# The delta-rule inverse recorded in closed stretches on VectorE, with later filler instructions tied behind its end

## The chip, the core and the metric

One core of one Trainium2 chip runs the whole program. The metric is the device time of one execution in microseconds (us); the time of the kernel before is the median of three runs. Five engines work side by side, each through a queue of its own and in the order in which the program puts them there: PE (TensorE, matrix products), DVE (VectorE), ACT (ScalarE), POOL (GpSimd) and SP (which issues DMAs). An engine goes on to its next instruction only when the semaphores that this instruction waits for have arrived, so an instruction that waits also holds up everything behind it in its queue.

## What is computed

Two transformer blocks on 256 tokens of width 1024. The second block has a gated delta rule with four heads of 128, beside a pooling branch, and after it a layer that picks 16 of 16384 experts for each head (the top-k). What the change touches is the delta rule. For each chunk and head the reference inverts a unit lower triangular matrix made from keys, decays and gates, and uses the inverse in everything that follows:

```python
q = _l2norm(qkv[..., :DN_WIDTH].reshape(b, s, DN_HEADS, DN_HEAD_DIM))
k = _l2norm(qkv[..., DN_WIDTH:2 * DN_WIDTH].reshape(b, s, DN_HEADS, DN_HEAD_DIM))
...
a_mat = jnp.where(strict, jnp.einsum("bhnid,bhnjd->bhnij", k_beta, k) * decay, 0.0)
t_mat = lax.linalg.triangular_solve(eye + a_mat, jnp.broadcast_to(eye, a_mat.shape),
                                    left_side=True, lower=True)
w_vals = jnp.einsum("bhnij,bhnjd->bhnid", t_mat, v_beta)
...
v_new = wv - jnp.einsum("bhcd,bhde->bhce", kcd, state)
o = jnp.einsum("bhcd,bhde->bhce", qd, state) + jnp.einsum("bhij,bhje->bhie", attn_c, v_new)
```

The kernel works with two chunks of 128 tokens (`tb` 0 and 1) and four heads, so eight 128x128 matrices `N`.

## The kernel before

Weights come from HBM in tiles of 128x1024 fp32 (512 KB). `Stream` turns each into two tiles: `whi` (an ACT copy, L218) and `wlo` (raw minus `whi`, on DVE, L231). A projection then is 24 matmuls (8 slices, three products each, L374 to L376) with 256 columns. There are five tile pairs in this stage and four raw tiles; a raw tile is loaded again only when its `wlo` has been written.

The delta stage, from about 430 to 550 us, weaves two strands together. The **main strand** (`main`, L1502) is the delta rule itself. The **filler** (`filler`, L1445) is the work beside it: sixteen projections, in the order q, v, p (pooling) and z with four heads each, every one followed on DVE by an evacuation from PSUM (`ct`, L1302, `pp`, L1434, `zt`, L1415), three convolution taps (L1306) for q and v, and a last product (L1295). The projections' outputs go through three PSUM buffers, `pb`; the main strand's go through four, `pa`. `weave` (L272) runs a piece of `main` up to its next `yield`, takes from the yielded number how much filler is due, and runs that much of `filler`. This decides the order in which instructions are recorded and their priority; a list scheduler that knows dependences and priorities then puts each engine's queue in order, so an instruction recorded later can still stand earlier.

The main strand in its own order, with the lines that the prediction speaks of:

1. the decays `dec` (L1512 on PE, L1517 and L1518 on ACT), masked on POOL (L1519, L1545);
2. the sums of squares of the keys (squares L525 on ACT, L1377 on PE) and their inverse root `yk` (`rsqrt_steps`, L408: three DVE steps, then three Newton rounds, with `eng=G` on POOL, L442 to L445, four instructions each);
3. `byk` (L1530), its spread over partitions by PE (L463), the products k by k (L1535), the matrix `N` (L1541, L1544) on DVE;
4. `inverse16` (L606): the diagonal 16x16 blocks `dg` (L619 to L623 on DVE), their rows copied to all partitions by PE and ACT (`rep`, L630 and L632), fifteen forward substitution steps on DVE ("the solve", L637 and L640), and the block diagonal `Z` (L644 on ACT, L646 on DVE);
5. three rounds that double the inverted blocks (L1563, L1574 on PE, L1579 and L1584 on DVE), the products with q (L1593), the transposes of v and k (L1615, L1619), and the state and outputs (L1476, L1627, L1631, L1637, L1498, L1645, L1646);
6. the output projection of the pooling branch, which is filler too, from the first matmul of `yah` on; then the tail of the stage.

## Time and profile before

| | us |
|---|---|
| median of three runs (1387.05 to 1393.6) | 1387.48 |
| the profiled execution | 1386.37 |
| its span in the trace | 1384.3 |
| PE busy | 1337.0 |
| DVE busy | 993.3 |
| ACT busy | 678.5 |

The span is what the trace covers; the execution's own time is 2.07 us longer. A PE that is shown busy may still be at half its clock, so the granted clock (1.00 is 2.4 GHz, 0.50 is 1.2 GHz) is read beside it. The trace shows the end of a matmul only as a model of the pipeline; the distance from one start to the next is what a matmul costs in a row of them.

### The profile page before, as it was taken

What the parts mean: (1) busy time and instruction counts of PE and PEld (TensorE: products, weight loads), DVE (VectorE), ACT (ScalarE), POOL (GpSimd) and SP (SyncE); (2) the same over time, 40 slices, a digit from 0 to 9 for tenths busy, and PEclk for the clock granted to TensorE, in tenths of its full rate; (3) what the DMA queues carried; (4) which work ended last, traced back from release to release, by engine and by line L of the source; (5) the groups of instructions that cost most, each with busy time, mean ns of one, the idle gap of its engine ahead of it and who ended that gap; (6) DMA issues with size and microseconds to landing.
All of it is one profiled execution on the core that took longest, in us unless ns stands there. A gap on an engine that the chain in (4) does not pass through costs nothing.

```text
span 1384.3 us, 26929 instructions
## 1 busy us (share of the span) xinstructions
PE 1337.0 (97%) x10570; PEld 1252.3 (90%) x10570; DVE 993.3 (72%) x2088; ACT 678.5 (49%) x1248; POOL 238.1 (17%) x230
## 2 busy tenths in 40 slices
PE   7989999999999968999999999999999999999998
PEld 6888988999989968999999999999998888888886
DVE  7865777898878975699995777888865555545554
ACT  3522455565565531465554554444444554554454
POOL 4611242100014610200000000000012222222221
PEclk9899999999999989999999999999999999999999
DMA  6241443565543311445555454545456555555553
GB/s 227 55 112 48 130 145 122 190 228 183 184 152 112 130 64 33 138 151 178 180 182 175 158 164 158 167 157 165 164 187 198 191 190 197 196 189 194 197 193 111
DMA packets 64335, 217.89 MB, mean 157 GB/s; under 512 B 10273, under 2 KB 11249, under 8 KB 64081
## 3 DMA queue, kind: packets, MB, share of 16 engines
q1 hardware_dynamic: 59376, 212.76, 46.1%
q0 software_dynamic: 992, 2.72, 0.7%
q8 instruction: 83, 1.36, 0.4%
q10 hardware_dynamic: 3840, 0.70, 0.4%
q14 instruction: 44, 0.35, 0.1%
HBM read 214.70 MB, written 1.44 MB: 156 GB/s over the span
## 4 chain that ended last, share of the span: by engine, by line
PE 86%; DVE 7%; ACT 3%; POOL 2%; issue 1%; DMA 1%; ACTq 0%; DVEq 0%; POOLq 0%
PE pa L1943 25%; PE pb L374 14%; PE pb L375 14%; PE pb L376 14%; PE pa L375 3%; PE pa L374 3%; PE pa L376 3%; PE pc L1897 1%; PE pb L1897 1%; PE pa L1574 1%; ACT whi L218 1%; DVE wlo L231 1%; PE pa L1064 1%; PE pb L1831 0%; PE pc L471 0%
## 5 line engine op out<-in xcount | busy, mean ns | idle before, releaser
L218 ACT ACTIVATE whi<-raw 128x1024 fp32r<-128x1024 f32 x396 | 418.3, 1058 | 509.4 <-PE pb L375 248.0
L231 DVE TENSOR_TENSOR wlo<-raw,whi 128x1024 fp32r<-128x1024 f32 x382 | 472.2, 1237 | 247.4 <-ACT whi L218 246.1
L374 PE MATMUL pb<-xnh,whi 128*128 128x256 f32 x1024 | 294.8, 288 | 0.0
L375 PE MATMUL pb<-xnl,whi 128*128 128x256 f32 x1024 | 290.1, 283 | 0.0
L376 PE MATMUL pb<-xnh,wlo 128*128 128x256 f32 x1024 | 289.5, 283 | 0.0
L1943 PE MATMUL pa<-whi,up 128*128 128x512 f32 x1024 | 274.7, 390 | 0.0
L1943 PEld LDWEIGHTS pa<-whi,up 128*128 128x128 f32 x1024 | 192.2, 188 | 39.8
L375 PEld LDWEIGHTS pb<-xnl,whi 128*128 128x128 f32 x1024 | 196.3, 192 | 0.0
L374 PEld LDWEIGHTS pb<-xnh,whi 128*128 128x128 f32 x1024 | 196.1, 192 | 0.0
L376 PEld LDWEIGHTS pb<-xnh,wlo 128*128 128x128 f32 x1024 | 196.0, 192 | 0.0
L374 PE MATMUL pb<-xh,whi 128*128 128x256 f32 x648 | 187.4, 289 | 0.0
L375 PE MATMUL pb<-xl,whi 128*128 128x256 f32 x648 | 184.8, 285 | 0.1
L376 PE MATMUL pb<-xh,wlo 128*128 128x256 f32 x648 | 184.9, 285 | 0.0
L1943 PE MATMUL pa<-wlo,up 128*128 128x512 f32 x512 | 158.4, 389 | 0.0
L511 POOL TENSOR_TENSOR up<-hb,up 128x256 fp32r<-128x256 f32 x32 | 45.9, 1435 | 553.8 <-ACT up L510 553.8
L374 PEld LDWEIGHTS pb<-xh,whi 128*128 128x128 f32 x648 | 124.1, 191 | 0.9 <-ACT xh L576 0.2
L375 PEld LDWEIGHTS pb<-xl,whi 128*128 128x128 f32 x648 | 123.9, 191 | 0.8 <-DVE xl L577 0.3
L376 PEld LDWEIGHTS pb<-xh,wlo 128*128 128x128 f32 x648 | 123.6, 191 | 0.5 <-DVE wlo L231 0.2
L1943 PEld LDWEIGHTS pa<-wlo,up 128*128 128x128 f32 x512 | 96.2, 188 | 19.9
L511 POOL TENSOR_TENSOR up<-scr,up 128x256 fp32r<-128x256 f32 x32 | 47.1, 1472 | 127.0 <-ACT up L510 127.0
L231 POOL TENSOR_TENSOR wlo<-raw,whi 128x1024 fp32r<-128x1024 f32 x19 | 46.4, 2448 | 45.1 <-ACT whi L218 35.2
L375 PE MATMUL pa<-al,whi 128*128 128x256 f32 x176 | 49.1, 281 | 0.0
(541 smaller groups left out, 2207.1 us busy)
## 6 DMA issues: line engine op xcount, KB each, us to landing
raw<-down SPq DMA_DIRECT2D x128, 512.0 KB, 3.3
raw<-up SPq DMA_DIRECT2D x128, 512.0 KB, 3.3
raw<-w_in SPq DMA_DIRECT2D x46, 512.0 KB, 3.4
raw<-w_up SPq DMA_DIRECT2D x44, 512.0 KB, 3.4
raw<-w_down SPq DMA_DIRECT2D x22, 512.0 KB, 3.4
raw<-w_out SPq DMA_DIRECT2D x16, 512.0 KB, 3.3
raw<-w_query SPq DMA_DIRECT2D x16, 512.0 KB, 3.4
x<-xT SPq DMA_DIRECT2D x4, 256.0 KB, 5.5
```

The costliest lines, as they stand in the source:

```text
L218: nc.scalar.activation(hi, self.raw[self.nh], AF.Copy)
L231: e.tensor_tensor(lo[:, a:z], raw[:, a:z], hi[:, a:z], ALU.subtract)
L374: mm(ps, w[0], x[0], start=start, stop=False, **k)
L375: mm(ps, w[0], x[1], start=False, stop=False, **k)
L376: mm(ps, w[1], x[0], start=False, stop=stop, **k)
L511: (eng or self.nc.vector).tensor_tensor(lo, src, hi.bitcast(F32), ALU.subtract)
L1064: mm(out[h, q], lh[h, 8 * hf + q, 0:64], self.halves(rh[h, 8 * hf + q, :], l, odd), start=True, stop=True)
L1574: mm(out[:, h], lh[:, tb * 4 + h, :], self.halves(rh[:, tb * 4 + h, :], l, odd), start=True, stop=True)
L1897: mm(ps[:, n, :], e1[:, q, :, r], eg[m][:, q, :, r], start=(m == 0), stop=(m == 1))
L1943: mm(acc[tb * 2 + hf], a[:, ts], b[:, hf * 512:hf * 512 + 512], start=False, stop=(e == 127 and lo == 1), skip_group_check=True)
```

## The change

`rsqrt_steps` loses its POOL variant, and `main` calls the DVE variant without yielding, as one piece; one `yield` after the k by k products goes too. The fifteen solve steps are one piece, with a single `yield` behind them where there were fifteen. `inverse16` keeps the last DVE instruction of two stretches (`self.blocks`: the sum that ends `dg`, then the last reduction of the solve), and `weave` records each piece of filler that follows inside `tc.issue_after` of that instruction: every DVE instruction of such a piece gets an order behind it. Other engines' instructions get none. The first entry of `YL`, the filler due after each piece of `head`, goes from 0.2 to 0.45. No arithmetic changes but the form of the Newton rounds.

```diff
-YL = [0.2, 0.64, 1.60, 3.20, 0.64, 0.72, 0.48, 0.80, 0.40, 1.92, 1.20, 0.16]
+YL = [0.45, 0.64, 1.60, 3.20, 0.64, 0.72, 0.48, 0.80, 0.40, 1.92, 1.20, 0.16]
...
-def weave(tc, main, fill, engines="", lead=None, leads=None):
+def weave(tc, main, fill, engines="", lead=None, leads=None, behind=None):
...
             while debt > 0:
-                g = next(fill, None)
+                with tc.issue_after(behind[0]) if behind else ExitStack():
+                    g = next(fill, None)
...
-        if eng:
-            v = v if mult else src
-            for _ in range(3):
-                yield pace
-                eng.tensor_tensor(t, v, y, ALU.mult)
-                eng.tensor_tensor(t, t, y, ALU.mult)
-                eng.tensor_scalar(t, t, -0.5, 1.5, ALU.mult, ALU.add)
-                eng.tensor_tensor(y, y, t, ALU.mult)
-            return y
...
-        V.tensor_tensor(dg, dg, dg2, ALU.add)
+        self.blocks = V.tensor_tensor(dg, dg, dg2, ALU.add).ins
...
-                V.tensor_reduce(zd[:, h, j:j + 1], tmp[:, h, 0:j + 1], mybir.AxisListType.X, ALU.add)
-            yield 0.6
+                last = V.tensor_reduce(zd[:, h, j:j + 1], tmp[:, h, 0:j + 1], mybir.AxisListType.X, ALU.add)
+        self.blocks = last.ins
+        yield 0.6
...
-                yield from self.rsqrt_steps(ss[:, 0:8], 8, 1.0, 4e-6, out=yk, pace=YL[11], eng=G)
+                self.rsqrt(ss[:, 0:8], 8, 1.0, 4e-6, out=yk)
...
-                yield YL[1]
                 for tb in range(2):
                     bb = b4(self.pa())
...
                 next(inv)
+                behind.append(self.blocks)
                 yield YL[2]
                 next(inv)
                 yield YL[3]
+                next(inv)
+                behind[0] = self.blocks
                 for w in inv:
                     yield YL[4]
...
-            weave(tc, main(), fl, MAIN, LEAD3)
+            weave(tc, main(), fl, MAIN, LEAD3, behind=behind)
```

How this moves the queues. In the rows below an output stands left of the arrow and the inputs right of it, and the line numbers of the changed kernel are a few lower than those of before (L630 is L622 there, L1563 is L1560, L374 to L376 are L375 to L377).

PE, before: the end of the sixteen projections (`pb`), and the inverse behind all of them.

```order
L374 MATMUL pb<-xh,whi 128x256
L375 MATMUL pb<-xl,whi 128x256
L376 MATMUL pb<-xh,wlo 128x256
L630 MATMUL pa<-dg,sel 128x128 x16
L1563 MATMUL pa<-con_base,Z 128x128 x8
L1574 MATMUL pa<-TT,N 128x64 x8
L1593 MATMUL pa<-q,k 128x128 x7
```

PE, changed: the same `rep` matmuls (L622), now behind only six of the projections.

```order
L375 MATMUL pb<-xh,whi 128x256
L376 MATMUL pb<-xl,whi 128x256
L377 MATMUL pb<-xh,wlo 128x256
L1530 MATMUL pa<-k 128x128 x8
L1370 MATMUL pc<-ones,sq 128x1 x12
L455 MATMUL pa<-con_base,byk 128x128 x8
L622 MATMUL pa<-dg,sel 128x128 x16
L1370 MATMUL pc<-ones,sq 128x1 x2
L375 MATMUL pb<-xh,whi 128x256
```

From the k by k products to the `rep` matmuls no projection stands on PE any more; the other ten moved behind: v's heads 2 and 3 and p's head 0 between `rep` and L1560 (L1563 of before), and seven between the later steps of the inverse.

DVE, before: the diagonal blocks `dg`, with pieces of filler (weight splits, z, pooling) between their instructions.

```order
L621 SCALAR_TENSOR_TENSOR dg<-N,con_del,dg 128x128
L1295 SCALAR_TENSOR_TENSOR z<-th,zt 128x256
L621 SCALAR_TENSOR_TENSOR dg_5775<-N,con_del,dg_5775 128x128
L1415 TENSOR_TENSOR zt<-pb,rbs 128x256
L231 TENSOR_TENSOR wlo<-raw,whi 128x1024
L621 SCALAR_TENSOR_TENSOR dg<-N,con_del,dg 128x128
```

DVE, changed: the end of the same stretch and the beginning of the solve.

```order
L613 SCALAR_TENSOR_TENSOR dg_5834<-N,con_del,dg_5834 128x128
L615 TENSOR_TENSOR dg<-dg,dg_5834 128x128
L1288 SCALAR_TENSOR_TENSOR q<-th,q 128x256
L231 TENSOR_TENSOR wlo<-raw,whi 128x1024
L1295 TENSOR_TENSOR ct<-pb,rbs 128x256
L231 TENSOR_TENSOR wlo<-raw,whi 128x1024
L1295 TENSOR_TENSOR ct<-pb,rbs 128x256
L1299 SCALAR_TENSOR_TENSOR q<-ct,params,q 128x255
L629 TENSOR_TENSOR itmp<-zd,rep 128x4x2 x2
```

The stretch from the inverse root to the sum of `dg` holds no filler now; six pieces of it stand between that sum and the first solve step.

DVE, before: the end of the solve, `Z`, and the first products of the doubling rounds.

```order
L637 TENSOR_TENSOR itmp<-zd,rep 128x64 x2
L640 TENSOR_REDUCE zd<-itmp 128x4 x2
L646 TENSOR_SCALAR Z<-zd,con_del 128x8x16 x4
L1584 TENSOR_TENSOR Y<-pa,con_del 128x16x16 x2
L1596 SCALAR_TENSOR_TENSOR att<-pa,yk,dec 128x128 x4
```

DVE, changed: the same place.

```order
L632 TENSOR_REDUCE zd<-itmp 128x4 x2
L1299 SCALAR_TENSOR_TENSOR v<-ct,params,v 128x254
L231 TENSOR_TENSOR wlo<-raw,whi 128x1024
L1295 TENSOR_TENSOR ct<-pb,rbs 128x256
L231 TENSOR_TENSOR wlo<-raw,whi 128x1024
L639 TENSOR_SCALAR Z<-zd,con_del 128x8x16 x4
L1295 TENSOR_TENSOR ct<-pb,rbs 128x256
```

Four pieces of filler stand between the solve and `Z`, and about twenty more between `Z` and the first `Y`.

## Rows read from the trace of the kernel before

**Rows 1.** The page: the span, and the chain that ended last by engine.

```profile
span 1384.3 us, 26929 instructions
PE 86%; DVE 7%; ACT 3%; POOL 2%; issue 1%; DMA 1%; ACTq 0%; DVEq 0%; POOLq 0%
```

**Rows 2.** Windows: stretch, length, busy us and instructions by engine, granted clock, DMA.

```profile
470.00:480.00 10.00, 7.15 (x46) 6.74 (x45) 7.75 (x20) 4.35 (x11) 8.76 (x18) 0.83 0.49 158
500.00:510.00 10.00, 3.44 (x16) 3.25 (x17) 6.37 (x36) 2.45 (x6) 1.99 (x2) 0.52 0.00 0
```

**Rows 3.** Waits of PE from 425 to 570 us: total, times, longest.

```profile
PE pa L1563 <- DVE Z L646: 8.8, 1, 8.8
PE pb L1468 <- POOL rt L443: 2.9, 1, 2.9
PE pb L1468 <- DVE pw L1440: 1.9, 1, 1.9
PE pa L1627 <- DVE vn L1623: 0.8, 1, 0.8
```

**Rows 4.** Windows: behind the second of these waits, and of the chain behind the first.

```profile
473.60:476.50 2.90, 2.90 (x12) 2.72 (x13) 2.24 (x5) 1.07 (x4) 2.74 (x6) 0.50 0.72 215
506.50:535.00 28.50, 27.08 (x204) 26.15 (x204) 12.69 (x33) 2.38 (x4) 0.00 (x0) 0.87 0.00 1
```

**Rows 5.** Timeline of PE: start, length (pipelined), instruction, passes, idle before.

```profile
443.92 0.37 PE L374 MATMUL pb<-xh,whi 128*128 128x256 f32 x1
...
449.04 0.28 PE L374 MATMUL pb<-xh,whi 128*128 128x256 f32 x1
...
451.92 0.28 PE L374 MATMUL pb<-xh,whi 128*128 128x256 f32 x1
454.68 1.95 PE L1535 MATMUL pa<-k 128*128 128x128 f32 x16
457.18 1.84 PE L1377 MATMUL pc<-ones,sq 128*128 128x1 f32 x16
...
479.79 1.04 PE L463 MATMUL pa<-con_base,byk 128*128 128x128 f32 x8
...
494.05 3.73 PE L630 MATMUL pa<-dg,sel 128*128 128x128 f32 x32
535.48 0.36 PE L374 MATMUL pa<-yah,whi 128*128 128x256 f32 x1
```

**Rows 6.** Timelines of ACT and DVE: the strand from the key squares to `byk`.

```profile
453.66 1.38 ACT L525 ACTIVATE sq<-k 128x256 f32<-128x256 f32 x4
462.33 0.22 DVE L424 TENSOR_SCALAR rv<-pc 128x4 f32<-128x4 f32 x2
478.10 0.68 DVE L1530 TENSOR_TENSOR byk<-beta,yk 128x8 f32<-128x8 f32 x1 [1.55 <-POOL yk L445]
```

**Rows 7.** Timeline of DVE: Newton steps of an earlier root, `N`, `dg`, fillers, solve, `Z`.

```profile
42.22 0.24 DVE L450 TENSOR_TENSOR rt<-rv,ry 128x8 f32<-128x8 f32 x2
42.42 0.24 DVE L453 SCALAR_TENSOR_TENSOR rt<-rt,ry 128x8 f32<-128x8 f32 x2
...
481.96 1.27 DVE L1541 SCALAR_TENSOR_TENSOR N<-pa,N 128x512 f32<-128x512 f32 x2
483.16 2.14 DVE L1544 SCALAR_TENSOR_TENSOR N<-pa,yk,N 128x128 f32<-128x128 f32 x8
...
492.10 0.28 DVE L623 TENSOR_TENSOR dg<-dg,dg 128x128 f32<-128x128 f32 x1
492.35 1.22 DVE L231 TENSOR_TENSOR wlo<-raw,whi 128x1024 fp32r<-128x1024 f32 x1
493.49 0.42 DVE L1295 SCALAR_TENSOR_TENSOR z<-th,zt 128x256 f32<-128x256 f32 x1
...
496.69 0.25 DVE L637 TENSOR_TENSOR itmp<-zd,rep 128x8 f32<-128x8 f32 x2
...
504.45 1.96 DVE L646 TENSOR_SCALAR Z<-zd,con_del 128x128 f32<-128x128 f32 x4
```

More of the change, by code (lines that the diff above doesn't have):

```diff
@@ L406, in rsqrt, with rsqrt_steps @@
         return drive(self.rsqrt_steps(*a, **k))
-    def rsqrt_steps(self, src, n, mult, add=None, floor=None, out=None, pace=0.2, eng=None):
+    def rsqrt_steps(self, src, n, mult, add=None, floor=None, out=None, pace=0.2):
         nc, sm = self.nc, self.s1
@@ L1500, in sums @@
                                        ALU.mult, ALU.add)
+            behind = []
             def main():
```

## The prediction

> **What bounds the kernel now.** I read the page first. PE is on 86% of the chain that ended last, DVE on 7%, in a span of 1384.3 us [rows 1]. So the question is where PE loses time. The windows of the delta stage name the place: from 500 to 510 us PE is busy for 3.44 of 10 us, at a granted clock of 0.52, and from 470 to 480 for 7.15, at 0.83; DVE works 6.37 and 7.75 us there [rows 2]. The waits of PE say for what: 8.8 us for `Z` at the end of the solve, 2.9 and 1.9 us for the pooling sums behind POOL and DVE, 0.8 us for `vn` [rows 3]. The first wait comes because the sixteen projections have run out before the solve begins. The second comes while POOL runs the Newton rounds of the key root between pooling sums. Behind both, PE works at half its clock: 2.9 us at 0.50 after the second, and 0.87 on average over the 28.5 us after the first [rows 4].
>
> This gives a ledger for PE from 443.92 us, up to where its queue is the same in both kernels, to 535.48 us, the first matmul of the pooling branch's output projection [rows 5]; from there on the two queues run alike again, but for a few exchanged places. Lost in before: 8.8 + 2.9 + 1.9 + 0.8 = 14.4 us of waiting, 2.9 x 0.5 = 1.45 us to half clock at 473.6, and 28.5 x 0.13 = 3.7 us to it after 506.5. Together 19.55 us. The rest, 91.56 - 19.55 = 72.0 us, is work at full clock (with a few short waits), which the change does not shrink. What the change is worth is 19.55 us minus what PE loses in the new order.
>
> **The change, part by part.** I replay the new queues with the durations of before, in three stretches.
>
> *Stretch A, up to `rep`.* On PE 57 projection matmuls stand before the k by k products: what is left of q, and v's heads 0 and 1. One projection of 24 takes 451.92 - 449.04 = 2.88 us [rows 5], so 57 take 6.8 us and end at 450.7. Then nothing but the main strand follows. The key squares on ACT ended at 453.66 + 1.38 = 455.0 in before [rows 6], with the decays in front of them; the decays are the same, one tap copy goes and a `tanh` and a `whi` take its place, so I leave them there and the sums on PE at 455.2. The root is now 12 pairs on DVE; an earlier root of the same kind goes from one pair to the next in 0.20 us [rows 7], so 2.4 us, then two small products: 458.0. Before, this took from 462.33 to 478.10 [rows 6]. PE spreads `byk` in 1.04 us for 8 [rows 5], of which the first four count, at half clock perhaps: 458.9. Then `N`, 483.16 - 481.96 = 1.2 and 2.1 us, to 462.2; and nine operations on `dg` at up to 0.28 each [rows 7], some pipelined: 464.5. Before, `dg` ended at 492.4: the chain is 28 us earlier here. The price: PE had 13.8 us from 450.7 to 464.5 and did 1.95 us of k by k, 24 passes of sums at 1.84 / 16 = 0.115 and 1.0 us of spreading, in all 5.7 us. **Lost: 8.1 us**, where before lost nothing. Nothing hides it, since the projections stand behind in PE's queue.
>
> *Stretch B, `rep` and the solve.* Two branches meet at L1563. On DVE six filler pieces come first: two splits at 493.49 - 492.35 = 1.14 us, four short ones at about 0.35 (0.42 with its tail) [rows 7]: 3.7 us, so the solve starts at 468.2. By then the first copy of `rep` is there: PE makes all four in 3.73 us at full clock and 7.5 at half [rows 5], and the solve needs a later copy only every fourth step. (On ACT these copies are queued behind the square of q's head 2, which now waits for its product, the first filler behind `dg`; that wait ends 0.4 us after `dg`, before PE's first group.) The solve took from 496.69 to 504.4 [rows 7], 7.7 us; five short fillers and `qe`, which waits for PE's sums of q, are inside now: +1.7. It ends at 477.6, 26.8 us earlier than before. Then four fillers, 1.14 + 1.14 + 0.7 = 3.0 us, and `Z`, 1.96 us in before [rows 7] and less where POOL is quiet: 482.2. On PE the branch is `rep`, the last sums, v's heads 2 and 3, and p's head 0. That head needs the PSUM buffer of v's head 1, and the copy that frees it is the third filler behind the solve: 477.6 + 1.9 = 479.5. So PE waits there again, about 2.6 us, close to the 2.9 us that brought half clock before; with 1.45 us for it the head ends at 479.5 + 2.88 + 1.45 = 483.8. I take this branch: L1563 at 483.8. Its bounds are 482.2, where DVE ends, and 485.3, with the head all at half clock. PE's work in the 19.3 us is 3.7 + 0.9 + 3 x 2.88 = 13.3 us. **Lost: 6.0 us.**
>
> Here a page speaks against the change. What the rows show is that the clock stands at 0.50 behind a wait of 2.9 us and behind one of 8.8 us. The Trainium skill, page "TensorE: Matmul & The Clock Gate", section "HAM oscillation — how this bites in real kernels", says that a matmul loop with idle gaps between its bursts starts each burst at half rate, and advises to close the gaps; the new order opens three. The trace agrees with the half rate. By that rule each of the three bursts, `rep` with v, p's head, and the chain's start, would be slow, and the gain would be nearer that of the second rival below.
>
> *Stretch C, the chain.* The 46.2 us of work left (72.0 - 6.8 - 5.7 - 13.3) include seven projections that used to be done already. Where before waited for `rep` and `vn` with nothing else in the queue, a projection stands between now. Each step of the chain on DVE has fillers in front; the tightest is the first `Y`, behind some twenty fillers, about 9.5 us by the prices above, while PE has about 10.2 us of its own work up to the place that needs it. So I take 0.5 us, and bound it by 0 and by the third rival. **Lost: 0.5 us.**
>
> *No price.* The POOL rounds go: 12 instructions off an engine that nothing else waits for then. The raw loads on SP wait for `wlo`, and the splits of p's heads now stand behind `dg` and the solve; the loads that hang on them are four tiles ahead of PE, and each split is done before its projection in the replay. If that cover went, a late load would show as PE waiting for `wlo`.
>
> *Sum.* 8.1 + 6.0 + 0.5 = 14.6 us lost instead of 19.55: 5.0 us less. The profiled execution would go from 1386.37 to 1381.4 (span 1379.3). It lies 1.1 us under the median, so against 1387.48 I predict **1382.5 us**. What a measurement can tell from no change is 0.5%, 6.9 us: below 1380.6 is faster, above 1394.4 slower.
>
> **Rivals.** *The clock comes back in time.* If PE's half clock ends inside `rep` and the 2.6 us gap does not bring it back, DVE sets L1563, at 482.2 or, with `Z` short and the squares a little earlier, 481: 1.6 to 2.8 us more, and C may lose nothing: 0.5 more. That is a gain of 7 to 8.5 us: 1379.7, at the best 1378. For it: a wait of 1.9 us [rows 3] left no half clock to be seen in these rows. Against it: three gaps in a row. *The clock stays low.* If PE stays at 0.50 from A until some microseconds into C, then `rep` ends at 472, the two heads of v at 482.6, p's head at 488.3, and four more microseconds go in C: 488.3 + 46.7 + 4 = 539.0 instead of 535.5, 1388 to 1391. It decides once half clock lasts beyond 488. Against it: behind 8.8 us of waiting, the longest here, the loss was 3.7 us, so about 7.4 us of work at half clock [rows 4], and this needs over 20. I put it, with its milder forms from 1384.5 on, together. *DVE becomes the bound of the chain.* Place: C, where nine hand-overs to PE (`Y`, `TT`, `Z`, `vn`, `Sx`) each stand behind splits and taps. Price: if each makes PE wait for one split, 1.14 us, that is 10.3 us; for two, 20.5. In place of the 0.5 us of C that gives 1392.3 and 1402.5; the sign turns from the fifth lost split on (5.5 / 1.14). For it: DVE had 12.69 busy us in these 28.5 [rows 4] and now gets the fillers too. Against it: a projection or part of one stands between most of these steps on PE.
>
> **How the numbers follow.** Forecast, 1380.6 to 1384.5: 0.47. Clock in time, 1377.5 to 1380.6: 0.30. Clock low, 1384.5 to 1391: 0.14. DVE the bound: 0.09, of which 0.05 lies above 1394.4. Hence faster 0.30, same 0.65, slower 0.05. The range of 8 in 10 leaves out the best of the second case and what is above the middle of the third: 1377.5 to 1388.5.
>
> **What would show it.** Right: PE nearly idle from about 452 to 464 at falling clock; `dg` at about 464.5; the solve's last reduction near 478; a short gap of PE before p's head 0; L1563 at 482 to 485; the first `yah` matmul at about 530.5. Wrong: key squares much later than 455 (all of A moves), a solve held up for `rep` or for `qe`, waits of PE for `wlo`, `Y` or `TT` in the chain, or a change behind 540 us, where I expect only the shift.

## The result, and the profile after

The changed kernel takes 1380.99 us (median of five runs, 1380.43 to 1382.27); the kernel before, beside it, 1388.47. The ratio is 0.995, with a 95% interval of 0.9931 to 0.997. That is a gain of 7.5 us on the medians, just at the bound of 0.5%, and 5.7 us on the two profiled spans. The prediction was 1382.5 us in a range of 1377.5 to 1388.5, with "within 0.5%" the likeliest.

The span on the page of the changed kernel, against 1384.3 us [rows 1]:

```profile
span 1378.6 us, 26927 instructions
```

The waits of PE from 425 to 570 us (total, times, longest) answer to [rows 3]:

```profile
PE pa L622 <- DVE dg L615: 5.5, 1, 5.5
PE pb L375 <- DVE ct L1295: 3.5, 1, 3.5
PE pb L455 <- DVE yo L448: 2.6, 1, 2.6
PE pc L1370 <- ACT sq L517: 1.0, 1, 1.0
PE pa L455 <- DVE byk L1525: 0.5, 1, 0.5
```

None of the four waits of before is left: not `Z`, not the two pooling sums, not `vn`. In their place stand a wait of 5.5 us for `dg`, in front of `rep`, and one of 3.5 us for `ct`, the copy that frees a PSUM buffer, in front of p's head 0. The wait for `yo` lies at the end of the stage; before had 2.03 us there.

The windows of the three stretches A, B and C of the prediction, the last one in two parts (stretch, length, busy us and instructions of PE, PE's loads, DVE, ACT and POOL, granted clock, share and GB/s of DMA), answer to [rows 2, 4]:

```profile
450.70:464.50 13.80, 8.07 (x53) 7.34 (x51) 8.62 (x43) 4.86 (x12) 5.14 (x4) 0.70 0.00 0
464.50:483.80 19.30, 14.15 (x104) 13.98 (x105) 19.27 (x86) 8.10 (x16) 3.14 (x3) 0.86 0.23 78
483.80:506.50 22.70, 22.70 (x196) 22.59 (x196) 20.64 (x48) 10.61 (x24) 9.44 (x10) 1.00 0.38 121
506.50:535.00 28.50, 28.50 (x245) 28.39 (x245) 17.83 (x45) 8.63 (x16) 3.30 (x5) 1.00 0.28 93
```

From 483.8 to 535 us PE is busy without a gap at full clock, where before had it busy for 27.08 of 28.5 us at 0.87 in the same chain. The loss has moved to the front: in the first two stretches PE works 22.2 of 33.1 us. There DVE has the load, 19.27 of 19.3 us in the second.

PE's timeline through these stretches answers to [rows 5] (start, length, instruction, passes, idle before it and what ended it):

```profile
451.07 1.95 PE L1530 MATMUL pa<-k 128*128 128x128 f32 x16
454.00 1.95 PE L1370 MATMUL pc<-ones,sq 128*128 128x1 f32 x16 [0.99 <-ACT sq L517]
458.73 1.97 PE L455 MATMUL pa<-con_base,byk 128*128 128x128 f32 x8 [0.52 <-DVE byk L1525]
466.19 5.57 PE L622 MATMUL pa<-dg,sel 128*128 128x128 f32 x32 [5.50 <-DVE dg L615]
...
481.86 0.39 PE L375 MATMUL pb<-xh,whi 128*128 128x256 f32 x1 [3.46 <-DVE ct L1295]
...
484.83 1.04 PE L1560 MATMUL pa<-con_base,Z 128*128 128x128 f32 x8
...
529.64 0.37 PE L375 MATMUL pa<-yah,whi 128*128 128x256 f32 x1
```

The first `yah` matmul starts at 529.64 us instead of 535.48 [rows 5]: 5.84 us earlier, and that is the whole gain, since the spans differ by 5.7. The spread of `byk` and `rep` show PE at half clock, `rep` in part: 1.97 us for what takes 1.04 at L1560, and 5.57 for what took 3.73 before.

DVE's timeline of the key root, `dg` and the solve answers to [rows 6, 7]:

```profile
455.98 0.23 DVE L425 TENSOR_SCALAR rv<-pc 128x4 f32<-128x4 f32 x2 [2.46 <-PE pc L1370]
...
465.75 0.29 DVE L615 TENSOR_TENSOR dg<-dg,dg 128x128 f32<-128x128 f32 x1
...
469.62 0.25 DVE L629 TENSOR_TENSOR itmp<-zd,rep 128x8 f32<-128x8 f32 x2
...
472.28 1.42 DVE L629 TENSOR_TENSOR itmp<-zd,rep 128x20 f32<-128x20 f32 x2
...
479.61 0.34 DVE L632 TENSOR_REDUCE zd<-itmp 128x4 f32<-128x64 f32 x2
479.86 0.47 DVE L1299 SCALAR_TENSOR_TENSOR v<-ct,params,v 128x254 f32<-128x254 f32 x1
...
482.86 0.87 DVE L639 TENSOR_SCALAR Z<-zd,con_del 128x128 f32<-128x128 f32 x4
```

The root begins at 455.98; `dg` ends at 466.04 instead of 492.4 [rows 7]; the solve runs from 469.62 to 479.95; four filler pieces, from 479.86 to 482.86, stand between it and `Z`.

**A measure for the experiments.** Times of kernels that differ by one or two us cannot be told apart by their intervals, and the rest of the program, 1254 us, varies by as much. So the table also has the length of the delta stage in the profiled execution: from the first matmul of the gates to the first of the output projection of the delta rule (`oh`). It is the length in one execution and holds what PE lost to half clock in it: the kernels "root alone" and "no tie" below have the same waits and differ by 4.1 us in it (last section). These are the two ends in the timeline of before, and then of the changed kernel, 129.3 and 123.9 us apart:

```profile
424.69 0.28 PE L374 MATMUL pa<-xh,wbh 128*8 128x256 f32 x1
...
553.96 0.39 PE L374 MATMUL pa<-oh,whi 128*128 128x256 f32 x1
```

```profile
424.83 0.28 PE L375 MATMUL pa<-xh,wbh 128*8 128x256 f32 x1
...
548.72 0.58 PE L375 MATMUL pa<-oh,whi 128*128 128x256 f32 x1
```

Each ratio is to runs of before beside that kernel, with medians from 1387.25 to 1388.47 us; the medians are of 5 runs for the changed kernel and for `Z` first, of 8 for the head's fill, and of 12 for the others.

| kernel | median us | ratio to before (95%) | stage us |
|---|---|---|---|
| before | 1388.47 | | 129.3 |
| changed | 1380.99 | 0.995 (0.9931 to 0.997) | 123.9 |
| root alone | 1389.77 | 1.0007 (0.9985 to 1.0028) | 131.6 |
| no tie | 1388.85 | 1.0006 (0.998 to 1.0031) | 135.7 |
| tie behind `dg` alone | 1386.16 | 0.9983 (0.9961 to 1.0005) | 129.2 |
| tie behind the solve alone | 1384.81 | 0.9969 (0.9945 to 0.9994) | 127.9 |
| root on POOL again | 1384.86 | 0.9982 (0.9963 to 1.0) | 127.8 |
| head's fill 0.2 | 1381.4 | 0.9952 (0.993 to 0.9974) | 125.9 |
| PE kept busy | 1382.67 | 0.9965 (0.9938 to 0.9992) | 124.6 |
| copies left free | 1383.39 | 0.9963 (0.994 to 0.9986) | 126.9 |
| `Z` first | 1379.4 | 0.9945 (0.9932 to 0.9958) | 125.0 |
| filler under the wait for `dg` | 1383.37 | 0.9983 (0.9971 to 0.9994) | 128.8 |
| two splits on POOL | 1383.02 | 0.9964 (0.9941 to 0.9987) | 126.5 |
| more filler ahead | 1382.37 | 0.9963 (0.9939 to 0.9986) | 125.6 |

### The profile page after: what moved, and what is told of

The parts are those of the page before. It is cut to its first block, busy times and chain, and to the rows that moved or that the text cites. A ratio compares the mean times of both kernels' runs of the same rounds, so it can differ in the third digit from the quotient of the medians.

```text
span 1378.6 us, 26927 instructions
## 1 busy us (share of the span) xinstructions
PE 1334.4 (97%) x10570; PEld 1250.5 (91%) x10570; DVE 990.2 (72%) x2106; ACT 679.5 (49%) x1248; POOL 235.9 (17%) x218
## 4 chain that ended last, share of the span: by engine, by line
PE 64%; DVE 2%; ACT 0%; issue 0%; ACTq 0%; DVEq 0%
PE pa L1940 25%; PE pb L375 11%; PE pb L376 11%; PE pb L377 11%; PE pc L1894 1%; PE pb L1894 1%; PE pa L1571 1%; PE pa L375 1%; PE pa L376 1%; PE pa L377 1%; PE pb L1828 0%; DVE itmp L629 0%; DVE wlo L231 0%; DVE zd L632 0%; PE pa L1850 0%
## 5 line engine op out<-in xcount | busy, mean ns | idle before, releaser
L375 PE MATMUL pb<-xnh,whi 128*128 128x256 f32 x1024 | 294.3, 288 | 0.0
L376 PE MATMUL pb<-xnl,whi 128*128 128x256 f32 x1024 | 289.7, 283 | 0.0
L377 PE MATMUL pb<-xnh,wlo 128*128 128x256 f32 x1024 | 289.0, 283 | 0.0
L376 PEld LDWEIGHTS pb<-xnl,whi 128*128 128x128 f32 x1024 | 196.1, 191 | 0.0
L375 PEld LDWEIGHTS pb<-xnh,whi 128*128 128x128 f32 x1024 | 195.9, 191 | 0.0
L377 PEld LDWEIGHTS pb<-xnh,wlo 128*128 128x128 f32 x1024 | 195.7, 191 | 0.0
L375 PE MATMUL pb<-xh,whi 128*128 128x256 f32 x648 | 186.7, 288 | 3.5 <-DVE ct L1295 3.5
L376 PE MATMUL pb<-xl,whi 128*128 128x256 f32 x648 | 184.4, 285 | 0.1
L377 PE MATMUL pb<-xh,wlo 128*128 128x256 f32 x648 | 184.3, 284 | 0.0
L375 PEld LDWEIGHTS pb<-xh,whi 128*128 128x128 f32 x648 | 123.3, 190 | 4.5 <-DVE ct L1295 3.7
L376 PEld LDWEIGHTS pb<-xl,whi 128*128 128x128 f32 x648 | 123.3, 190 | 0.8 <-DVE xl L569 0.3
L377 PEld LDWEIGHTS pb<-xh,wlo 128*128 128x128 f32 x648 | 123.1, 190 | 0.3
L376 PE MATMUL pa<-al,whi 128*128 128x256 f32 x176 | 49.0, 281 | 0.0
```

The costliest lines, as they stand in the source:

```text
L375: mm(ps, w[0], x[0], start=start, stop=False, **k)
L376: mm(ps, w[0], x[1], start=False, stop=False, **k)
L377: mm(ps, w[1], x[0], start=False, stop=stop, **k)
```

## Which part of the change brings the gain

Two theories stood against each other at first. By mine the gain comes from the place of the chain: it stands some 26 us earlier, so that ten projections cover the solve and the rounds behind it, and the tie is what moves it. The rivals were that the Newton rounds off POOL make it, since their wait and the half clock behind it are 4.35 us, or that closed stretches do so without a tie.

**The root alone.** The kernel before, with one call changed:

```diff
-                yield from self.rsqrt_steps(ss[:, 0:8], 8, 1.0, 4e-6, out=yk, pace=YL[11], eng=G)
+                self.rsqrt(ss[:, 0:8], 8, 1.0, 4e-6, out=yk)
```

> The kernel before, with the root of the keys on DVE in one piece and the POOL rounds gone; everything else (woven stretches, no tie, head fill 0.2) as before. Theory (the gain of 5.8 us comes from the chain standing about 28 us earlier, so that ten projections cover the solve and the rounds behind it): the rep products still stand behind all sixteen projections here, so nothing covers the solve; the waits for the pooling sums (2.9 us) go, but the DVE works as much as before, so Z comes no earlier and the wait for Z grows from 8.8 to 10 to 14 us: 1386 to 1389. Rival (the root makes it: the 2.9 us wait behind POOL and its 1.45 us of half clock are 4.35 of the 5.8 us): 1382 to 1384.

**No tie.** The changed kernel, with the tie taken out:

```diff
-            weave(tc, main(), fl, MAIN, LEAD3, behind=behind)
+            weave(tc, main(), fl, MAIN, LEAD3)
```

> The changed kernel without the tie: closed stretches, root on DVE and head fill 0.45 stay, filler may again be scheduled anywhere. Theory (the tie is what moves the inverse ahead of ten projections): the queue of PE is that of before again, rep behind all sixteen projections, with a wait for Z of 8 to 14 us: 1386 to 1390. Rival (recording the stretches closed is enough, since DVE runs them without interruption): Z wait under 4 us, 1380 to 1383.

Nothing is gained by either, in time or in the stage. The longest waits of PE in the same stretch, with the root alone:

```profile
PE pa L1563 <- DVE Z L646: 8.8, 1, 8.8
PE pb L1468 <- DVE rt L453: 3.7, 1, 3.7
PE pb L1468 <- ACT th L1293: 2.8, 1, 2.8
```

The kernel without the tie has the same three, 8.8, 3.7 and 2.8 us. Both have the wait for `Z` of before to the tenth [rows 3], and both still wait for pooling sums, now behind DVE and ACT. Both rivals fall. My expectation for the root alone had the missing gain right (1389.77 us lies 0.8 above its range), but not its parts: I had the pooling waits gone and the wait for `Z` at 10 to 14 us. Without the tie `rep` stands behind all sixteen projections, whatever the root runs on.

**One tie at a time.** In the first kernel below filler stays tied behind `dg` and is never tied behind the solve; in the second it is free up to the end of the solve:

```diff
                 next(inv)
-                behind[0] = self.blocks
```

> The changed kernel with the first tie alone: filler stays tied behind the sum of dg, and is not tied behind the solve any more. In its queue of PE the stretch up to rep is as in the changed kernel, but then all ten projections stand ahead of the product with Z and none behind it. Theory (both ties are needed: the first to bring dg early, the second to keep the splits and taps from standing in the solve): the solve is stretched by filler until the projections run out, the chain behind it is bare again, and PE waits 3 to 9 us for Z beside the 8 us lost ahead of rep: 1384 to 1390. Rival (the first tie alone carries the gain, since ten projections cover the solve): 1380 to 1382.

```diff
                 next(inv)
-                behind.append(self.blocks)
...
-                behind[0] = self.blocks
+                behind.append(self.blocks)
```

> The changed kernel with the second tie alone: filler is free until the end of the solve and tied behind it then. In its queue of PE 48 projection matmuls more (5.8 us) stand ahead of rep than in the changed kernel, and only one projection (2.9 us) between rep and the product with Z. Theory (the loss is moved, not removed: what no longer idles ahead of rep idles behind it): PE waits 5 to 8 us between rep and Z and about 2 us ahead of rep; 1379 to 1383, within 2 us of the changed kernel. Rival (without the first tie filler on DVE holds dg back as before): 1385 to 1389.

With the first tie alone no gain clear of the noise is to be seen. With the second alone there is a part of it. The intervals of both ratios overlap the changed kernel's, so the times do not settle the order; the stages are 5.3 and 4.0 us longer. PE's timeline with the first tie alone:

```profile
501.61 1.19 PE L1461 MATMUL pb<-pw,wpl 128*128 128x256 f32 x2 [2.76 <-DVE pw L1433]
...
508.98 1.04 PE L1559 MATMUL pa<-con_base,Z 128*128 128x128 f32 x8
```

The wait for `dg` is there as in the changed kernel (5.5 us), and then all the projections run ahead of `Z`: the product with it starts at 508.98, 24 us later than in the changed kernel. The time came out in my range, but not by the wait that I named: PE does not wait for `Z` at all, because the projections last until then. It loses 1.6 and 2.8 us to pooling sums, since DVE has what they need between steps of the solve, runs at half clock behind the second (0.50 up to 504.6), and waits again for `vn`, 0.8 us, in a bare chain.

With the second tie alone the waits are these:

```profile
PE pb L375 <- DVE ct L1295: 6.8, 1, 6.8
PE pa L622 <- DVE dg L615: 5.5, 1, 5.5
```

The wait for `dg` is as long as before, although 48 projection matmuls more were done ahead of it; behind `rep` the next projection needed a buffer, and PE waited 6.8 us for the copy that frees it. Behind that wait it ran 5.4 us at half clock, 2.7 us lost. My theory (the loss is only moved, within 2 us) was too low. The median, 1384.81 us, lies 0.2 below the rival's range, but its mechanism (`dg` held back as before) fell: `rep` starts at 470.37 us, where before had 494.05 [rows 5]. Neither tie alone brought all of the gain in these executions, but 2.7 of the second's 4.0 us are clock.

**The root back on POOL**, with everything else kept (the `eng=G` branch of `rsqrt_steps` and its call as in the diff of the change):

> The changed kernel with the three Newton rounds of the key root on POOL again, everything else kept. Theory: PE is idle in this stretch and nothing hides it, so each us of the root's chain costs one. A round on POOL took 1.5 us when POOL was quiet before (469.94 to 471.47), three 4.6 us; on DVE nine pairs of 0.20 are 1.8 us. So dg ends about 3 us later and the kernel takes 2 to 4 us longer than the changed one: 1383 to 1385. Rival (DVE is the bound in the closed stretch and gets 1.8 us off, or the wait is hidden): within 1 us of the changed kernel, 1380 to 1382.

The stage is 3.9 us longer than in the changed kernel, as my theory had it, and so are the medians. Two of its waits:

```profile
PE pb L375 <- DVE ct L1304: 3.9, 1, 3.9
PE pa L464 <- DVE byk L1534: 2.4, 1, 2.4
```

But the parts differ. The wait for `byk` is 1.9 us longer and the one for `ct` 0.4; the first round on POOL took 1.13 us here (455.97 to 457.10), not 1.53. Most of the rest is clock: behind the wait for `ct` PE ran 5.4 us at 0.50, 2.7 us lost, which the changed kernel did not lose behind its own. So the rounds on DVE are worth 1.5 to 2 us in the closed stretch; the other half of the difference need not be theirs (last section).

**The head's fill back at 0.2:**

```diff
-YL = [0.45, 0.64, 1.60, 3.20, 0.64, 0.72, 0.48, 0.80, 0.40, 1.92, 1.20, 0.16]
+YL = [0.2, 0.64, 1.60, 3.20, 0.64, 0.72, 0.48, 0.80, 0.40, 1.92, 1.20, 0.16]
```

> The changed kernel with the fill after each piece of head at 0.2 as before instead of 0.45; 48 projection matmuls (5.75 us) that stood ahead of the k by k products now stand behind them. Theory: the solve and the chain are covered already (PE was never idle from 484 to 535 in the changed kernel), so what is missing ahead turns into idle time of PE in the closed stretch unless the key squares come earlier by as much; I take 2 us earlier and 3.5 us lost: 1384.5, between 1381 and 1387. Rival (the amount of head fill is without effect, it is only moved): 1380 to 1382.

By the time no difference can be measured: 1381.4 us, in the rival's range and at the low end of the theory's. By the stage the changed kernel is 2.0 us shorter. Two of the three longest waits of PE, beside the 5.5 us for `dg`:

```profile
PE pa L455 <- DVE byk L1525: 4.8, 1, 4.8
PE pc L1370 <- ACT sq L517: 3.9, 2, 2.8
```

PE idles more, as I had expected: 4.3 us more for `byk` and 2.9 more for squares, of the keys and then of q. What I had not seen is that most of it comes back. The projections that were not done ahead of the chain are done behind it, and PE no longer waits for `ct` (3.5 us) and for `yo` (2.6 us). Nor do the 2.0 us of the stage speak for the higher fill: behind the second wait for squares PE did 6.2 us of work at 0.50, up to 483.5, so 3.1 us were lost to the clock that the changed kernel did not lose there.

## What bounds the new order

In every kernel with a tie so far PE waits 5.4 to 5.5 us for `dg`. The next six ask whether that, the half clock there, and the 3.5 us for `ct` can be had back.

**PE kept busy.** Matmuls of zeros fill PE's idle time in the closed stretch; their results are read by nobody. The ties set their place:

```diff
+                with tc.issue_after(last.ins):      # behind the sums of the key squares
+                    self.clock_up(self.pc()[:, 0:T], 18)
...
+                with tc.issue_after(last.ins):      # behind the spread of byk
+                    self.clock_up(self.pc()[:, 0:T], 56)
```

> The changed kernel with 74 matmuls of zeros added on PE where it is idle: 18 behind the sums of the key squares, 56 behind the spread of byk, so that the clock is not lowered there. Their results are read by nobody. Theory (the stretch is bound by DVE, so half clock costs only what it adds to the spread, about 0.5 us of N's 0.88 us wait; rep's 1.8 us is hidden behind the six filler pieces ahead of the solve, and the wait for ct grows instead): 1379.5 to 1381. Rival (half clock is paid in full: 0.9 us of spread, 1.8 us of rep, 0.6 us of sums): 1377 to 1378.5.

The median lies above both expectations, and its interval (1378.6 to 1386.1 us against the 1387.25 beside it) takes in the theory's range and begins just above the rival's; the trace says more. PE's timeline:

```profile
456.00 3.81 PE L459 MATMUL pc<-idle 128*128 128x256 f16 x18 [0.33 <-DVE rv L425]
459.65 1.03 PE L455 MATMUL pa<-con_base,byk 128*128 128x128 f32 x8
460.52 6.44 PE L459 MATMUL pc<-idle 128*128 128x256 f16 x56
466.80 3.73 PE L622 MATMUL pa<-dg,sel 128*128 128x128 f32 x32
...
484.67 1.03 PE L1565 MATMUL pa<-con_base,Z 128*128 128x128 f32 x8
```

`rep` runs at full clock, 3.73 us instead of 5.57, and yet the product with `Z` comes 60.0 us after the stage's start (424.66), exactly as in the changed kernel (424.83 to 484.83). So the half clock of `rep` is free: the solve begins behind DVE's filler pieces at 469.39 here and at 469.62 in the changed kernel. For `rep`, its largest term, the rival fell, as the theory had it. For the spread the run decides nothing. The clock stood at 0.50 under most of the first 18 zeros (456.0 to 459.5), and they held the spread up to 459.65, though `byk` was there at 458.40. So `N` waited 1.55 us instead of 0.88, and `dg` came 0.3 us later after the stage's start, not earlier. What the half clock of the spread costs, which the theory put at 0.5 us, was not measured.

**Copies left free.** Only splits, taps and last products are tied; the copies from PSUM are not:

```diff
-                    if f:
-                        f()
+                    if f:
+                        with tied(f):
+                            f()
...
+            def tied(f=None):
+                return tc.issue_after(behind[0]) if behind and f not in free else ExitStack()
...
-                S.split(eng)
+                with tied():
+                    S.split(eng)
```

> The changed kernel with the tie on the splits, taps and last products alone; the evacuations of projections from PSUM (ct, zt, pp) may be scheduled ahead of dg and of the solve's end. In its queue of PE 52 projection matmuls more (6.2 us) stand ahead of rep, and 68 instead of 72 between rep and the product with Z. Theory (PE's two large waits of the changed kernel, 5.5 us for dg and 3.5 us for ct, are there because the copies that free the three PSUM buffers are tied behind dg and the solve): both shrink to under 2 us, for some 0.4 us of DVE a copy in the closed stretches and a chain whose end is bare again (1 to 2 us): 1375 to 1379. Rival (DVE is the bound here; then the waits come back for dg, for Z or later in the chain): 1380 to 1383.

My theory falls; 1383.39 us lies 0.4 above the rival's range, and the waits come back as it said. The stage is 3.0 us longer than the changed kernel's, 1.7 of them half clock behind the second of these waits. The two longest waits of PE:

```profile
PE pa L622 <- DVE dg L615: 5.7, 1, 5.7
PE pb L377 <- DVE wlo L231: 5.2, 1, 5.2
```

The 52 projection matmuls that were freed went ahead of the spread, not behind it, so the wait for `dg` stayed; and the wait for a copy became one for a split that is tied behind the solve. The chain, bare in part, waits 1.9 us for `TT`.

**`Z` ahead of the filler.** The second tie stands behind the last DVE write of `Z` instead of the solve:

```diff
-        self.blocks = last.ins
-        yield 0.6
         for a in range(nb):
...
-                V.tensor_scalar(Z[:, :, 16 * a:16 * a + 16], zd, bm[:, a:a + 1], None, ALU.mult)
+                last = V.tensor_scalar(Z[:, :, 16 * a:16 * a + 16], zd, bm[:, a:a + 1], None, ALU.mult)
+        self.blocks = last.ins
```

> The changed kernel with the second tie behind the last write of Z on DVE instead of the last reduction of the solve. The four filler pieces that stood between the two in the changed kernel (a tap, two splits and ct, from 479.86 to 482.86: 3.0 us) go behind Z, and the product with Z moves ahead of the projection that waited for ct. Theory (DVE sets the end of the solve and of Z, and PE has other work only if its copies come in time): Z comes 3 us earlier, PE waits for it from 478.4 to 481 instead of for ct to 481.9, and that projection covers the rounds behind: 1 us there, and up to 2.5 us more if its work still lasts when the tail waits for yo: 1377 to 1380. Rival (the pieces pushed behind Z are late for the next step, so the wait reappears at Y, TT or a split): 1381 to 1384.

The median, 1379.4 us, is the lowest here and in the range of the theory, but the stage, 125.0 us, is 1.1 us longer than the changed kernel's; the rest of the program took 1253.1 us instead of 1254.7. So I don't call it faster. The timeline of POOL's memsets, `Z` on DVE, and the product on PE:

```profile
479.96 1.99 POOL L1555 MEMSET rep<- 128x1024 f32 x2 [6.30 <-DVE itmp L629]
...
480.13 1.96 DVE L637 TENSOR_SCALAR Z<-zd,con_del 128x128 f32<-128x128 f32 x4
...
482.24 1.94 PE L1559 MATMUL pa<-con_base,Z 128*128 128x128 f32 x8 [2.97 <-DVE Z L637]
```

`Z` starts 2.7 us earlier, as expected, but takes 1.96 us instead of 0.87, since POOL's memsets now run beside it. The product with `Z` comes 58.0 us after the stage's start instead of 60.0. Behind its wait of 2.97 us PE works at half clock up to 488.6, and these 6.4 us cost 3.2 us that neither theory had. The wait for `yo` is gone, as expected.

**Filler forced under the wait for `dg`.** The last two edits together, and a tie on PE behind the spread for all filler recorded later:

```diff
+                pes.append(last.ins)                # the last spread of byk
...
-            weave(tc, main(), fl, MAIN, LEAD3)
+            weave(tc, main(), fl, MAIN, LEAD3, behind=pes)
```

> The kernel of z_first with two more edits: the copies from PSUM are not tied on DVE, and on PE the filler recorded after the spread of byk is tied behind that spread, so that 56 projection matmuls (6.7 us) stand between the spread and rep, where PE waited 5.5 us for dg, and 96 between rep and the product with Z. Theory (what the closed stretch costs is PE's idle time, because the projections that could fill it wait for copies tied behind dg; DVE has room for a copy of 0.4 us there): the wait for dg falls from 5.5 to under 1 us and the wait for ct is gone, 5 to 8 us less than the changed kernel lost, of which 1 to 2 us come back as a later dg: 1374 to 1378. Rival (DVE is the bound of this stage as a whole, so filling PE earlier only moves its waits to a split (wlo) or to Z): 1380 to 1384.

The theory missed, the rival's range holds: 1383.37 us, a stage of 128.8. The two longest waits of PE in the stage, and then the windows at the two places where it loses:

```profile
PE pa L1539 <- DVE k L1294: 4.3, 1, 4.3
PE pa L1581 <- DVE Y L1591: 2.8, 1, 2.8
```

```profile
445.00:465.00 20.00, 16.17 (x80) 16.02 (x81) 12.99 (x59) 7.67 (x23) 5.28 (x4) 0.57 0.04 16
...
485.00:495.00 10.00, 7.25 (x61) 7.06 (x59) 10.00 (x18) 3.58 (x9) 4.08 (x4) 0.96 0.71 245
495.00:505.00 10.00, 10.00 (x49) 9.82 (x48) 7.89 (x25) 2.23 (x7) 1.90 (x3) 0.53 0.20 66
```

The wait for `dg` is gone, all 5.5 us of it. But the tie also took the projections away that used to stand ahead of the k by k products: PE waits 4.3 us for `k` there, and runs most of 445 to 465 at half clock, its projections too. DVE is busy for all of 485 to 495, and where the chain needs it, at `Y`, PE waits for it and runs at half clock again, up to 504.5. In this stage PE did 24.9 us of its work at half clock (12.5 us lost), in that of the kernel with `Z` first 17.0 (8.5 lost), while its waits come to 11.4 and 11.2 us. By this count the 3.8 us between the two stages are clock, and the run does not show that DVE bounds the stage.

**Two more ways to unload DVE**, both on top of the kernel with `Z` first. In the one, two splits go to POOL; in the other, more filler is due ahead of the closed stretch:

```diff
-                    ps = yield from fproj(DS[h % 2])
+                    ps = yield from fproj(G if name == "v" and h in (1, 2) else DS[h % 2])
```

> The kernel of z_first with the two weight splits that stand behind dg on DVE (the splits after v's heads 1 and 2) given to POOL, which is idle there; a split took 1.14 us on DVE and takes 2.4 us on POOL. Theory (DVE is busy without a gap from dg to Z and sets both; PE's waits there are its shadow): the solve starts 1.2 to 2.3 us earlier after dg (bounded by the first copy of rep), Z too, and PE's wait for Z falls from 3.0 to 1 to 2 us: 1377 to 1378.5. Rival (POOL's splits slow the DVE steps beside them, as the step of the solve beside POOL's egb took 1.42 us instead of 0.28): the distance from dg to Z stays within 0.5 us, 1379 to 1381.

```diff
-YL = [0.45, 0.64, 1.60, 3.20, 0.64, 0.72, 0.48, 0.80, 0.40, 1.92, 1.20, 0.16]
+YL = [0.45, 2.7, 1.60, 3.20, 0.64, 0.72, 0.48, 0.80, 0.40, 1.92, 1.20, 0.16]
```

> The kernel of z_first with more filler due after the sums of the key squares (2.7 instead of 0.64), so that DVE gets filler in the 4 us where it waits for the squares and sums (445 to 455), and 24 projection matmuls (2.9 us) more stand ahead of the k by k products. Theory (DVE is the bound from dg on, and work moved into its gap ahead of the closed stretch comes off that): PE's 1.0 us wait for the squares goes, dg comes 1 to 2 us later, and the distance from dg to Z shrinks by 2 us or more: 1376.5 to 1379. Rival (the gap cannot be used without delaying the squares on ACT, so all of the closed stretch moves by the whole 2.9 us): 1379.5 to 1382.

They take 1383.02 and 1382.37 us, with stages of 126.5 and 125.6: neither is better than the kernel that they start from. The timeline of DVE and POOL in the solve, with two splits on POOL:

```profile
476.81 2.59 DVE L629 TENSOR_TENSOR itmp<-zd,rep 128x44 f32<-128x44 f32 x2
...
476.85 2.47 POOL L231 TENSOR_TENSOR wlo<-raw,whi 128x1024 fp32r<-128x1024 f32 x1 [2.80 <-ACT whi L218]
```

The pair of steps beside POOL's split takes 2.59 us, where its neighbours take 0.40. Two pairs of the root, beside the other split and a mask on POOL behind it, take 0.87 and 1.25 us instead of 0.24. The wait for `byk` rises from 0.5 to 3.0 us and that for `Z` from 3.0 to 5.6. POOL is idle there, but not free. This is the rival's mechanism, and dearer than it said. It is no clean test of two splits less on DVE behind `dg`, since two splits still stood there: the scheduler had filled the places with others, and one of POOL's ran far ahead, at 453.46.

With more filler ahead, the stage's start lies at 425.77 instead of 424.29; counted from there, `rep` starts 0.8 us later than in the kernel with `Z` first (at 468.62 and 466.33) and the product with `Z` 0.8 us later too (at 484.49 and 482.24). The distance between them did not shrink: the wait for the squares went, as the theory had it, but filler moved ahead was replaced behind `dg`, where the numbers further on in the list set its amount. The theory's second half fell; the rival's 2.9 us were too many.

## Why the prediction was right, and where it was not

**The place and the size** were right, the size in part by luck. The ledger had PE lose 14.6 us in the new order; it lost 13.7 (529.64 - 443.92 - 72.0), and where 5.0 us were to be gained 5.84 came. But the two stretches ahead of the chain ended 1.0 us later than predicted and the chain took 1.9 us less, and inside the second stretch two larger errors cancel, as told below. That the earlier chain is what pays, and not POOL or the root, is shown by the kernel with the root alone and by the one without the tie.

**Stretch A** was predicted to end at 464.5; `dg` ended at 466.04. The squares began at 453.50 on ACT, 0.16 us earlier than in before. The step that was short is the one behind them: I had the root start with the sums at 455.2, and it started at 455.98. It took 2.45 us (2.4 predicted). Then the spread at half clock cost `N` a wait of 0.88 us, and the rest of `dg` half a microsecond more. PE waited 7.4 us there (5.5, 1.0, 0.5 and 0.4); the prediction had it idle for 8.1.

**Stretch B** was predicted to end at 483.8, within 482.2 and 485.3; it ended at 484.83. The six pieces ahead of the solve took 3.6 us from the end of `dg` (3.7 predicted), the four ahead of `Z` 2.9 (3.0). The solve took 10.3 us instead of 9.4: one step beside POOL's product for `egb` took 1.42 us. The buffer wait that I worked out as the bound is there, 3.5 us instead of 2.6 because DVE was later. The term that failed is the half clock behind it: I took 1.45 us from [rows 4], and the clock stayed at 1.00. So a delay of 2.3 us of DVE was offset by a loss that did not come; that the end still lay within the bounds is luck.

What the rule of the Trainium skill, page "TensorE: Matmul & The Clock Gate", section "HAM oscillation — how this bites in real kernels", made of this (each burst behind an idle gap starts at half rate) agrees with the first of the three bursts: `rep` ran at half clock until 470. But the clock had fallen already between 456 and 458 us (0.56 there), behind the sums of squares and two short waits of 1.0 and 0.4 us, and so ahead of the gap in front of `rep`. That rule does not hold for the second, p's head 0, and there was no third gap.

**Stretch C** was to take 46.7 us and took 44.8, with no wait of PE at all. The 0.5 us did not come: each projection in between did cover DVE's fillers, though DVE was busy for 20.64 of the first 22.7 us. The other 1.4 us were not work at full clock: the 72.0 us were a remainder, and before's PE was idle for 1.42 us of its 28.5 [rows 4], of which the ledger had named 0.8; waits of 0.3 us each for `rep` and `osq` are nearly all of the rest. Where the remaining 0.8 us lay in before was not traced.

**The rivals.** The likeliest case and "the clock comes back in time" met: the median, 1380.99, lies in the range of the first, 0.4 us from the second's. The condition of the second held in B (half clock ended inside `rep`, and the wait did not bring it back), and C lost nothing, as it said. What it drew from that for B did not come: p's head 0, which waited for its buffer, and not `Z` set the product at 484.83. Its arithmetic slipped too: a gain of 7 to 8.5 us gives 1379.0 to 1380.5, not "at the best 1378". The case "the clock stays low" did not come in the changed kernel, but variants of it show 5 to 7 us of work at half clock behind the wait in B. DVE did not become the bound of the chain; ahead of it, from `dg` to `Z`, DVE is busy almost without a gap (19.27 of 19.3 us).

**What is shown and what is not.** Shown: the tie moves the chain, and without it nothing is gained; the half clock of `rep` costs nothing; the wait for `dg` can be filled, and the time does not fall, with as much waiting elsewhere and more work at half clock. In single executions only, with half clock in their sums: that each of the ties is needed. Not shown: that less work on DVE between `dg` and `Z` would shorten the stage. Two edits were to show it and neither took work off that stretch. Nor is it shown what the closed recording adds to the tie, since no kernel has the tie with the stretches still woven, or what the half clock of the spread costs.

## What to carry to other kernels

Closing a stretch on one engine and tying other work behind it pays by where it puts what stands behind it on the other engines; here the closed stretches without the tie gained nothing (ratio 1.0006). So ask which engine runs out of work first, before and after, and what is then left for it at the end of the chain. Filler that is moved forward or backward mostly moves the idle time (the head's fill at 0.2: 7.2 us more in two waits, 6.1 us less in two others), so price both ends. An engine that looks idle in the profile is not free for a helper's work if a DVE chain on the path runs beside it.

## What the runs showed of the hardware

Whether PE's clock is low behind a wait of some 3 to 4 us is not settled by the wait's length, nor by PE's queue. The kernel with the root alone and the one without the tie have the same queue of PE up to the second doubling round, and the same waits. PE behind the second pooling wait, start and window, with the root alone, and then without the tie:

```profile
489.02 0.67 PE L1468 MATMUL pb<-pw,wpl 128*128 128x256 f32 x2 [2.82 <-ACT th L1293]
...
490.00:497.00 7.00, 7.00 (x62) 7.00 (x61) 5.93 (x16) 3.63 (x7) 0.92 (x1) 1.00 0.38 119
```

```profile
490.18 1.19 PE L1461 MATMUL pb<-pw,wpl 128*128 128x256 f32 x2 [2.82 <-ACT th L1286]
...
490.00:500.00 10.00, 9.82 (x58) 9.67 (x59) 6.14 (x16) 3.13 (x6) 1.72 (x1) 0.68 0.20 58
```

Behind the same 2.82 us PE went on at 1.00 in the one and at 0.68 on average over 10 us in the other. (Over the 7 us from 490 to 497 the second stood at 0.55.) So also between the other kernels: 1.00 behind 3.46 us (changed) and 3.62 us (PE kept busy), 0.50 behind 2.97 us (`Z` first) and 3.87 us (root on POOL). A term for half clock behind such a wait was zero or, where the clock fell, 1.45 us ([rows 4]) to 5.1 us (10.2 us of work behind the wait of 2.75 us for `Y` in the filler under `dg`). What chooses between them is open. It is a caution for all stage lengths above, each of one execution: the root alone did 10.6 us of PE's stage at half clock and the kernel without the tie 20.0, half of which is lost; that makes 4.7 us, where their stages differ by 4.1.

Some DVE instructions beside one of POOL lasted until POOL was done. `Z` took 1.96 us beside POOL's memsets, and 0.87 us without them in the changed kernel; a pair of solve steps took 2.59 us instead of 0.40 beside POOL's split. Not all do: a split on DVE took its 1.22 us beside the memsets, at 480.25 in the changed kernel. The long ones agree with the Trainium skill, page "SBUF — State Buffer", section "Who interferes with whom", which has the two engines share a pair of ports that one of them holds for its whole instruction. In before, too, `Z` took 1.96 us [rows 7], from 504.45 on, with the memsets from 504.28 to 506.27, which made DVE's part of `Z` 1.1 us longer. Of the 8.8 us wait for `Z` at most 0.7 us was theirs, since ACT's part ended at 505.73 and DVE's at 506.41. In the changed kernel they end at 481.65, ahead of `Z`, though no line of the change is about them.
